# Second expert product of a decoder step: expert rows as the moving operand, 512 columns at a time

## The chip, the cores and the metric

The kernel runs on one core of a Trainium2 chip. The metric is the device time of one execution in microseconds (us). Engines are named as in the profile: PE is TensorE (matmuls), PEld its weight loads, DVE is VectorE, ACT is ScalarE, POOL is GpSimd, SP is SyncE, whose queue issues the weight transfers.

## The reference

One layer of a decoder runs over 256 prompt tokens and 64 sample tokens (8 sequences of 8), with a model width of 2048. In outline:

```
h = x + W_out [ RMSNorm(attention(q,k,v)) ; RMSNorm(SGU(u,v)) ]
h = h + PEER(RMSNorm(h))
h = h + (p @ W_ple) * sigmoid(RMSNorm(h) @ W_gate)

def one_block(xb):                       # PEER
    ...                                  # 8 heads, top 16 of 128x128 experts -> e, softmax -> g
    ue  = take(u_tab, e)                 # 16384 experts, 2048 wide
    act = gelu(einsum('thkd,td->thk', ue, xb))
    ve  = take(v_tab, e)
    return einsum('thk,thkd->td', g * act, ve)
```

The change is in the last line, the sum over experts of `g * act` times the expert's row in `v_tab`, for the 256 prompt tokens.

## The kernel before

Everything is f32 and is kept transposed: model dimensions on the 128 partitions, tokens along the free axis. `hT` holds h as 16 chunks of 128 dimensions by 320 tokens (256 prompt, then 64 sample). A weight unit is 1 MB (128 x 2048 f32); `unit` loads it through SP's queue into one of three `w_raw` buffers, and `split` makes a high part (`w_hi`, ACT, line 77) and a low part (`w_lo`, DVE, line 78) of each half of it, four buffers each, so that two units lie ready ahead of PE. `mm3` (lines 87 to 91) does a product as three matmuls: high by high, high by low, low by high. `hilo` splits an activation in the same way.

For the prompt tokens the experts are not gathered. The first product, `u_unit`, computes all 16384 activations, one unit of 128 experts at a time. Its later form (lines 612 and 613) streams the high and the low half of x in one matmul of 512 columns, and then 256 columns against `w_lo`. `weights` multiplies the activations with the dense routing weights, which are zero for experts not chosen, and splits them into `wh` and `wl`: 128 experts on partitions, 256 tokens along the free axis.

The second product, `v_group`, runs 16 times, each time for 8 units of 128 experts. It has 8 units of expert rows, each with two blocks of 128 model dimensions. For each block 24 matmuls add up in one PSUM tile `ps_o`: the expert rows are the stationary operand, 256 columns of `wh` or `wl` move. DVE then adds the tile to `hT` (line 786). Between two groups lie six or seven units of the first product.

The 64 sample tokens do gather: `c_step` fetches a row per token and choice with an indirect transfer on POOL's queue (tile `row`, two buffers) and works it up on DVE (lines 735 and 743), paced so that all 128 steps are issued when the last group starts; `add_samples` turns the sum back with matmuls against `stack` (line 772). After the last group come the per-layer embedding (`ps_s`, 96 matmuls of 320 columns, line 825 copies it out), the norm of h (`hilo` and a sum of squares for each of the 16 chunks, lines 109, 114, 133 and 134), and the gate product of 16 units.

The order of instructions on each engine is set by a scheduler with a cost model of its own, not by the program's order alone: at the start of the last group, for instance, the matmuls of `add_samples` stand among those of `ps_o`, and the norm's work on chunk after chunk stands among the products of the last group. PSUM has four tags of two banks each: `mm`, `s`, `o`, `tr`.

Of the kernel before, what the change touches and what calls it, by code (L numbers as in the profile page):

```python
# [10 lines left out]
F32 = mybir.dt.float32  # L11
# [5 lines left out]
AF = mybir.ActivationFunctionType  # L17
# [3 lines left out]
P = 128  # L21
D = 2048
NC_ = D // P
TP = 256
# [9 lines left out]
GRP = 8  # L34
NG = NK // GRP
# [13 lines left out]
def _build(ctx, tc, nc, a):  # L49
    vec, act, pool, pe = nc.vector, nc.scalar, nc.gpsimd, nc.tensor  # L50
# [5 lines left out]
    def shut(cm):  # L56
        cm.__exit__(None, None, None)
# [4 lines left out]
    ps = ctx.enter_context(tc.tile_pool(name="ps", bufs=2, space=bass.MemoryType.PSUM))  # L62
    drm = ctx.enter_context(tc.tile_pool(name="drm", bufs=1, space=bass.MemoryType.DRAM))
    gd = drm.tile([NG, P, 16 * GRP * 16], F32, name="gd")

    def psum(tag, cols, parts=P):
        t = ps.tile([P, 512], F32, tag=tag, name="ps_" + tag)
        return t[:parts, :cols]


    def split(src, lo_eng=None):
        out = []
        for h in range(2):
            hi = hl.tile([P, 8, P], F32R, name="w_hi")
            lo = hl.tile([P, 8, P], F32R, name="w_lo")
            s = src[:, 8 * h : 8 * h + 8]
            act.activation(hi, s, AF.Copy)  # L77
            (lo_eng or vec).tensor_sub(lo, s, hi.bitcast(F32))  # L78
            out.append((hi, lo))
        return lambda c: (out[c // 8][0][:, c % 8], out[c // 8][1][:, c % 8])  # L80

    def unit(src, lo_eng=None):
        r = raw.tile([P, 16, P], F32, name="w_raw")
        nc.sync.dma_start(r.rearrange("p a b -> p (a b)"), src)
        return split(r, lo_eng)

    def mm3(out, w, xh, xl, start, stop):
        wh, wl = w
        pe.matmul(out, wh, xh, start=start, stop=False)  # L89
        pe.matmul(out, wh, xl, start=False, stop=False)  # L90
        pe.matmul(out, wl, xh, start=False, stop=stop)  # L91

    def dense(out, w, x, n=NC_):
        for c in range(n):
            mm3(out, w(c), *x(c), c == 0, c == n - 1)
# [33 lines left out]
    def square_sum(pool_, tot, x, first):  # L129
        if first:  # L130
            return act.activation(tot, x, AF.Square)
        sq = pool_.tile([P, T], F32, tag="sq", name="sq", bufs=2)
        act.activation(sq, x, AF.Square)
        return vec.tensor_add(tot, tot, sq)
# [14 lines left out]
    ident = cp.tile([P, P], F32, name="ident")  # L149
    hT = cp.tile([P, NC_, T], F32, name="hT")  # L150
# [86 lines left out]
    for b4 in range(2):  # L237
        pt = psum("tr", 512)
# [225 lines left out]
    with tc.tile_pool(name="wo", bufs=2, reuse_waits="tile") as wo:  # L464

        early = [psum(tag, T) for tag in ("mm", "mm", "o", "o")]
        for half in range(2):
            for o2 in range(2):
                w = unit(a["w_out"][2 * half + o2])
                for k in range(2):  # L470
                    for c in range(8):
                        i = 8 * half + c
                        mm3(early[2 * o2 + k], w(8 * k + c), *xmix(i), i == 0, i == NC_ - 1)
        for o in range(NC_):
            xr = wo.tile([P, T], F32, name="xr", bufs=4)
            pool.dma_start(xr, a["xT"][o])
            if o < 4:
                pt = early[o]
            else:
                pt = psum("mm", T)  # L480
                dense(pt, unit(a["w_out"][o]), xmix)
            vec.tensor_add(hT[:, o], pt, xr)
            hilo(xh(o), hT[:, o], g_ffn[:, o : o + 1])
            square_sum(wo, ssq, hT[:, o], o == 0)
    shut(c_b)
    shut(c_a1)

# [24 lines left out]
    r = rstd(rt, pm[:, 0 : TP + 3], TP + 3)  # L512
# [68 lines left out]
    for n, h in enumerate((0, 4, 1, 5, 2, 6, 3, 7)):  # L581
        sp = [psum("s", 256), psum("tr", 256), psum("o", 256)]
        r0 = 64 * (h // 4)
        for half in range(2):
            pt = psum("mm", T)
# [131 lines left out]
    c_vp, vp = open_pool("vp")  # L717
# [30 lines left out]
    def paced():  # L748
        state["unit"] += 1
        while state["n"] < min(128, state["unit"] * 128 // N_UNITS):  # L750
            c_step()
# [15 lines left out]
    def add_samples():  # L767
        for c4 in range(2):
            pt = psum("tr", 512)
            for c in range(8):  # L770
                dt = 8 * c4 + c
                pe.matmul(pt[:, c * TS : c * TS + TS], acc[:, dt * P : dt * P + P], stack, start=True, stop=True)
            vec.tensor_add(
                hT[:, 8 * c4 : 8 * c4 + 8, TP:], hT[:, 8 * c4 : 8 * c4 + 8, TP:],
                pt.rearrange("p (c t) -> p c t", c=8),
            )

    def v_group(g, ws):
        for d2 in range(8):
            w = unit(a["v_t"][g, d2])  # L780
            for k in range(2):
                pt = psum("o", TP)
                for i in range(GRP):
                    mm3(pt, w(8 * k + i), *ws[i], i == 0, i == GRP - 1)
                dt = 2 * d2 + k
                vec.tensor_add(hT[:, dt, 0:TP], hT[:, dt, 0:TP], pt)
            paced()
            if g == NG - 1 and d2 == 1:
                add_samples()

    u_unit(U1, False)
    ws = weights(0)
    for e in range(U1 + 1, LEAD):
        u_unit(e, False)
    done = LEAD
    for g in range(NG):
        v_group(g, ws)
        if g + 1 < NG:
            upto = LEAD + (NK - LEAD) * (g + 1) // (NG - 1)
            while done < upto:  # L800
                if done == upto - 1 and upto < NK:
                    ws = weights(g + 1)
                u_unit(done, True)
                paced()
                done += 1
            if upto == NK:
                ws = weights(g + 1)
# [5 lines left out]
    with tc.tile_pool(name="pl", bufs=2, reuse_waits="tile") as pl:  # L813
# [17 lines left out]
        r = rstd(pl, pm, T)  # L831
        for o in range(NC_):
            pt = psum("mm", T)
# [55 lines left out]
def _layout(i):  # L889
    c = np.ascontiguousarray  # L890
    x = np.concatenate([i["x_prompt"][0], i["x_sample"].reshape(TS, D)], 0)
    p = np.concatenate([i["p_prompt"][0, 0], i["p_sample"][0].reshape(TS, -1)], 0)
    w_in = i["w_in"][0]

    order = np.concatenate([np.r_[j * HD : j * HD + HD, (8 + j) * HD : (9 + j) * HD] for j in range(NJ)])
    w_in = np.concatenate([w_in[:, order], w_in[:, 1024:]], 1)
    w_out = np.concatenate([i["w_out"][0][order], i["w_out"][0][1024:]], 0)

    first = w_out[:, :512].reshape(2, 8, P, 2, 2, P).transpose(0, 3, 2, 4, 1, 5).reshape(4, P, D)
    cols = lambda v: v.reshape(-1, P).T  # L900
    gains = np.concatenate(
        [cols(i["norm_mix"][0]), cols(i["norm_ffn"][0]), cols(i["ple_gate_norm"][0]),
         cols(i["attn_out_norm"][0][order]), cols(i["sgu_out_norm"][0]),
         np.tile(i["q_norm"][0], 2)[:, None], np.tile(i["k_norm"][0], 2)[:, None], i["sgu_norm"][0][:, None]], 1)
    sinks = i["sinks"][0].reshape(2, NJ)
    sw = i["sgu_w"][0]
    wS = np.zeros((DB, DS, SH, DB, DS), np.float32)
    for b in range(DB):
        wS[b, :, :, b, :] = sw[:, :DS, :DS].transpose(2, 0, 1)
    u, v = i["peer_u"][0], i["peer_v"][0]  # L910
    return {
        "xT": c(x.T).reshape(NC_, P, T),
        "gains": c(gains),
        "w_in": _units(w_in, 26),
        "w_out": c(np.concatenate([first, _units(w_out, 16)[4:]], 0)),
        "wq": _units(i["peer_wq"][0], 16),
        "w_gate": _units(i["ple_gate_w"][0], 16),
        "ple_w": c(i["ple_w"][0].reshape(2, P, 2, 8, P).transpose(2, 1, 3, 0, 4)).reshape(2, P, D),
        "pT": c(p.T.reshape(2, P, T).transpose(1, 0, 2)),
        "uT": c(u.reshape(NK, P, NC_, P).transpose(0, 3, 2, 1)).reshape(NK, P, D),  # L920
        "v_t": c(v.reshape(NG, GRP, P, 8, 2, P).transpose(0, 3, 2, 4, 1, 5)).reshape(NG, 8, P, D),
        "u_rows": u,
        "v_rows": v,
        "k12": c(np.stack([i["peer_k1"][0].T, i["peer_k2"][0].T], 1)),
        "ckT": c(i["cache_k"][0].transpose(2, 3, 0, 1)).reshape(P, DB, P),
        "cv": c(i["cache_v"][0].transpose(1, 0, 2, 3)).reshape(P, DB, P),
        "cache_k": i["cache_k"][0].reshape(DB, P, P),
        "cache_v": i["cache_v"][0].reshape(DB, P, P),
        "sink_p": c(np.broadcast_to(sinks.T.reshape(1, 16), (P, 16))),
        "sink_s": c(np.repeat(sinks.reshape(16), 8)[:, None]),  # L930
        "sgu_wT": c(sw.transpose(2, 0, 1)),
        "sgu_wS": wS.reshape(TS, SH, TS),
        "sgu_b": c(np.broadcast_to(i["sgu_b"][0][None], (P, SH, P))),
        "g_row": c(np.broadcast_to(i["sgu_norm"][0][None], (TS, P))),
        **_constants(),
    }
# [27 lines left out]
```

## Time and profile before

| | |
|---|---|
| time, median of 3 runs | 2170.55 us (2168.24 to 2172.44) |
| the profiled execution | 2172.83 us |
| its span, first to last instruction | 2171.1 us |
| granted PE clock, mean | 0.998 |
| busy: PE, DVE, ACT, POOL | 99%, 78%, 48%, 12% |
| traffic | 531.39 MB, mean 245 GB/s |

The span is what the views of the trace divide up; 1.7 us of the profiled execution lie outside it. Busy PE time counts a matmul from its start to its end, and matmuls overlap, so the pace of PE is read from start to start.

### The profile page before, as it was taken

How to read it: one execution, taken by the hardware profiler on the slowest of the kernel's cores; microseconds unless marked ns; L12 is line 12 of the kernel's file. 1: busy time of each engine (PE TensorE's matmuls, PEld its weight loads, DVE VectorE, ACT ScalarE, POOL GpSimd, SP SyncE). 2: the span in 40 equal slices, each digit the busy share in tenths (PEclk: the TensorE clock that was granted, in tenths of full speed). 3: DMA queues.
4: the chain of work that ended last, by engine and by line, in shares of the span. 5: the costliest groups of instructions: out<-in, count | busy, mean ns of one | idle time of the engine just before them, and what ended most of it. 6: DMA issues, size and time to landing. Idle time of an engine off the chain costs nothing.

```text
span 2171.1 us, 38182 instructions
## 1 busy us (share of the span) xinstructions
PE 2148.3 (99%) x15538; PEld 2039.2 (94%) x15538; DVE 1698.9 (78%) x2806; ACT 1034.7 (48%) x1543; POOL 263.4 (12%) x190
## 2 busy tenths in 40 slices
PE   7999999999999999999999999999999999999999
PEld 7778999999999999999999999999999999999999
DVE  6575875699988678888878888788888888788754
ACT  5246554335476644444445444444444444445632
POOL 3000000000001111111111111111212211111000
PEclk9999999999999999999999999999999999999999
DMA  7322355333567789788788878888788888886452
GB/s 266 133 78 81 104 199 179 138 117 136 176 193 238 225 312 342 293 316 317 300 316 315 309 289 318 307 323 321 289 321 303 305 310 317 299 317 253 172 178 85
DMA packets 80415, 531.39 MB, mean 245 GB/s; under 512 B 9094, under 2 KB 13622, under 8 KB 19424
## 3 DMA queue, kind: packets, MB, share of 16 engines
q1 hardware_dynamic: 50208, 350.80, 45.5%
q0 software_dynamic: 24912, 158.30, 19.5%
q10 hardware_dynamic: 5120, 19.86, 2.4%
q8 instruction: 122, 2.00, 0.4%
q14 instruction: 53, 0.43, 0.1%
HBM read 509.07 MB, written 20.84 MB: 244 GB/s over the span
## 4 chain that ended last, share of the span: by engine, by line
PE 89%; issue 5%; DVE 2%; DMA 1%; POOL 1%; ACT 0%; POOLq 0%; ACTq 0%; DVEq 0%
PE ps_mm L612 16%; PE ps_o L89 11%; PE ps_o L90 11%; PE ps_o L91 11%; PE ps_mm L90 8%; PE ps_mm L613 8%; PE ps_mm L89 8%; PE ps_mm L91 8%; PE ps_s L684 1%; POOL gd L694 1%; DVE w_lo L78 1%; DMA g_t<-gd 0%; PE ps_s L262 0%; PE ps_s L590 0%; DMA gd<-g_st 0%
## 5 line engine op out<-in xcount | busy, mean ns | idle before, releaser
L77 ACT ACTIVATE w_hi<-w_raw 128x1024 fp32r<-128x1024 f32 x664 | 703.0, 1060 | 927.4 <-PE ps_o L90 336.9
L78 DVE TENSOR_TENSOR w_lo<-w_raw,w_hi 128x1024 fp32r<-128x1024 f32 x664 | 808.8, 1223 | 253.5 <-ACT w_hi L77 249.7
L89 PE MATMUL ps_o<-wh,w_hi 128*128 128x256 f32 x2048 | 575.1, 281 | 0.6 <-ACT wh L109 0.6
L90 PE MATMUL ps_o<-wl,w_hi 128*128 128x256 f32 x2048 | 573.3, 280 | 1.0 <-DVE wl L112 1.0
L91 PE MATMUL ps_o<-wh,w_lo 128*128 128x256 f32 x2048 | 569.8, 278 | 0.3 <-DVE w_lo L78 0.3
L90 PEld LDWEIGHTS ps_o<-wl,w_hi 128*128 128x128 f32 x2048 | 385.0, 188 | 1.4 <-DVE wl L112 1.4
L89 PEld LDWEIGHTS ps_o<-wh,w_hi 128*128 128x128 f32 x2048 | 384.5, 188 | 1.6 <-ACT wh L109 1.0
L91 PEld LDWEIGHTS ps_o<-wh,w_lo 128*128 128x128 f32 x2048 | 385.0, 188 | 0.5 <-DVE w_lo L78 0.5
L89 PE MATMUL ps_mm<-a,w_hi 128*128 128x320 f32 (+1 forms) x1008 | 310.1, 308 | 9.0 <-ACT w_hi L77 8.9
L90 PE MATMUL ps_mm<-a,w_hi 128*128 128x320 f32 (+1 forms) x1008 | 311.9, 309 | 0.7 <-DVE a L114 0.7
L91 PE MATMUL ps_mm<-a,w_lo 128*128 128x320 f32 (+1 forms) x1008 | 308.1, 306 | 1.8 <-DVE w_lo L78 1.8
L612 PE MATMUL ps_mm<-a,w_hi 128*128 128x512 f32 x768 | 270.9, 392 | 0.0
L612 PE MATMUL ps_mm<-c,w_hi 128*128 128x512 f32 x768 | 270.8, 391 | 0.0
L613 PE MATMUL ps_mm<-c,w_lo 128*128 128x256 f32 x768 | 215.1, 280 | 0.0
L613 PE MATMUL ps_mm<-a,w_lo 128*128 128x256 f32 x768 | 215.1, 280 | 0.0
L89 PEld LDWEIGHTS ps_mm<-a,w_hi 128*128 128x128 f32 x1008 | 191.8, 190 | 14.4 <-ACT w_hi L77 9.1
L90 PEld LDWEIGHTS ps_mm<-a,w_hi 128*128 128x128 f32 x1008 | 192.0, 190 | 9.1 <-issue 7.6
L91 PEld LDWEIGHTS ps_mm<-a,w_lo 128*128 128x128 f32 x1008 | 191.6, 190 | 5.3 <-issue 2.6
L612 PEld LDWEIGHTS ps_mm<-c,w_hi 128*128 128x128 f32 x768 | 143.7, 187 | 31.8
L612 PEld LDWEIGHTS ps_mm<-a,w_hi 128*128 128x128 f32 x768 | 143.7, 187 | 31.3
L730 POOL DMA_INDIRECT row<-in_v_rows,c_e x64 | 111.3, 1740 | 496.2 <-DVE xc L743 440.6
L730 POOL DMA_INDIRECT row<-in_u_rows,c_e x64 | 101.1, 1580 | 509.3 <-DVE row L735 503.2
(338 smaller groups left out, 3144.2 us busy)
## 6 DMA issues: line engine op xcount, KB each, us to landing
w_raw<-in_uT SPq DMA_DIRECT2D x128, 1024.0 KB
w_raw<-in_v_t SPq DMA_DIRECT2D x128, 1024.0 KB
w_raw<-in_w_in SPq DMA_DIRECT2D x25, 1024.0 KB
w_raw<-in_w_out SPq DMA_DIRECT2D x16, 1024.0 KB
w_raw<-in_wq SPq DMA_DIRECT2D x16, 1024.0 KB
gd<-g_st POOLq DMA_DIRECT2D x16, 1024.0 KB, 6.1
g_t<-gd ACTq DMA_DIRECT2D x16, 1024.0 KB
w_raw<-in_w_gate SPq DMA_DIRECT2D x16, 1024.0 KB
```

The lines of the kernel that those rows point to most:

```text
L77: act.activation(hi, s, AF.Copy)
L78: (lo_eng or vec).tensor_sub(lo, s, hi.bitcast(F32))
L89: pe.matmul(out, wh, xh, start=start, stop=False)
L90: pe.matmul(out, wh, xl, start=False, stop=False)
L91: pe.matmul(out, wl, xh, start=False, stop=stop)
L612: pe.matmul(pt, wh, x(c), start=c == 0, stop=False)
L613: pe.matmul(pt[:, 0], wl, x(c)[:, 0], start=False, stop=c == NC_ - 1)
L684: pe.matmul(gp[:, t * P : t * P + P], e2[:, q, :, t], p[:, q, :, t], start=k == 0, stop=k == 1)
L694: pool.dma_start(gd[:, :, tb * P : tb * P + P].rearrange("g p x -> p g x"), st.rearrange("p (g i) t -> p g (i t)", g=NG),)
L730: pool.indirect_dma_start(out=row, out_offset=None, in_=tab, in_offset=bass.IndirectOffsetOnAxis(ap=c_e[:, j : j + 1], axis=0),)
```

## The change

The operands of the second product change places. Stationary is now a block of 128 experts by 128 tokens of `wh` or `wl`; moving are 512 model dimensions of the expert rows. Sums stand with tokens on partitions, and `hT`'s prompt columns serve as their accumulator: group 0 copies into it, groups 1 to 15 add. So h itself is written to DRAM (`hd`) when it is made, read back into the two `row` buffers at the start of the last group, and added to the sums when those are turned back by PE transposes (`h_back`), a quarter of the model width at a time. The rows in `v_t` are laid out anew; its units keep their size.

```diff
+    hd = drm.tile([2, P, 8 * TP], F32, name="hd")
...
-    def split(src, lo_eng=None):
+    def split(src, lo_eng=None, wide=1):
...
+        if wide > 1:
+            return lambda i: [x[:, i * wide % 8 : i * wide % 8 + wide].rearrange("p a b -> p (a b)") for x in out[i * wide // 8]]
...
             square_sum(wo, ssq, hT[:, o], o == 0)
+            if o % 8 == 7:
+                pool.dma_start(hd[o // 8], hT[:, o - 7 : o + 1, 0:TP])
...
+    def y_part(tt, dq):
+        return hT[:, 4 * dq : 4 * dq + 4, tt * P : tt * P + P]
+
+    def h_back(dq):
+        for c in range(4 * dq, 4 * dq + 4, 2):
+            pt = psum("tr", 512)
+            for k in range(4):
+                pe.transpose(pt[:, k * P : k * P + P], hT[:, c + k // 2, k % 2 * P : k % 2 * P + P], ident)
+            vec.tensor_add(
+                hT[:, c : c + 2, 0:TP], h_kept[c // 8][:, c % 8 : c % 8 + 2], pt.rearrange("p (c t) -> p c t", c=2)
+            )
+
     def v_group(g, ws):
-        for d2 in range(8):
-            w = unit(a["v_t"][g, d2])
-            for k in range(2):
-                pt = psum("o", TP)
-                for i in range(GRP):
-                    mm3(pt, w(8 * k + i), *ws[i], i == 0, i == GRP - 1)
-                dt = 2 * d2 + k
-                vec.tensor_add(hT[:, dt, 0:TP], hT[:, dt, 0:TP], pt)
-            paced()
-            if g == NG - 1 and d2 == 1:
-                add_samples()
+        for dq in range(4):
+            pt = [psum("o", 512), psum("s", 512)]
+            for ih in range(2):
+                w = unit(a["v_t"][g, 2 * dq + ih], wide=4)
+                for i in range(4):
+                    wh, wl = w(i)
+                    e = 4 * ih + i
+                    for tt in range(2):
+                        xh_, xl_ = [x[:, tt * P : tt * P + P] for x in ws[e]]
+                        pe.matmul(pt[tt], xh_, wh, start=e == 0, stop=False)
+                        pe.matmul(pt[tt], xl_, wh, start=False, stop=False)
+                        pe.matmul(pt[tt], xh_, wl, start=False, stop=e == GRP - 1)
+                paced()
+            for tt in range(2):
+                y, p = y_part(tt, dq), pt[tt].rearrange("p (c d) -> p c d", c=4)
+                if g == 0:
+                    act.activation(y, p, AF.Copy)
+                else:
+                    vec.tensor_add(y, y, p)
+            if g == NG - 1:
+                if dq == 0:
+                    add_samples()
+                h_back(dq)
...
     for g in range(NG):
+        if g == NG - 1:
+            h_kept = []
+            for k in range(2):
+                t = vp.tile([P, D], F32, tag="row", name="h_kept", bufs=2)
+                nc.scalar.dma_start(t, hd[k])
+                h_kept.append(t.rearrange("p (c t) -> p c t", c=8))
         v_group(g, ws)
...
-        "v_t": c(v.reshape(NG, GRP, P, 8, 2, P).transpose(0, 3, 2, 4, 1, 5)).reshape(NG, 8, P, D),
+        "v_t": c(v.reshape(NG, 2, 4, P, 4, 512).transpose(0, 4, 1, 3, 2, 5)).reshape(NG, 8, P, D),
```

## Rows read from the trace of the kernel before

**Rows 1.** The page: span, PE's busy time, and the chain that ended last.
```profile
span 2171.1 us, 38182 instructions
...
PE 2148.3 (99%) x15538; PEld 2039.2 (94%) x15538; DVE 1698.9 (78%) x2806; ACT 1034.7 (48%) x1543; POOL 263.4 (12%) x190
...
PE 89%; issue 5%; DVE 2%; DMA 1%; POOL 1%; ACT 0%; POOLq 0%; ACTq 0%; DVEq 0%
```

**Rows 2.** Busy time by stretch: group 0, group 8, units after it, group 15; sum of 1000:1900.
```profile
core 0: us, PE busy (x) PEld busy (x) DVE busy (x) ACT busy (x) POOL busy (x), PEclk, DMA share, GB/s
775.58:823.17 47.59, 45.98 (x385) 45.18 (x385) 45.05 (x72) 22.55 (x32) 5.25 (x4) 1.00 0.86 326
...
1422.91:1468.14 45.23, 45.23 (x387) 45.23 (x385) 37.95 (x42) 19.27 (x24) 10.19 (x6) 1.00 0.82 297
1468.14:1501.42 33.28, 33.28 (x194) 29.34 (x193) 27.47 (x34) 16.29 (x25) 5.05 (x3) 1.00 0.87 316
1989.14:2037.82 48.68, 48.68 (x418) 48.49 (x417) 43.10 (x69) 30.99 (x51) 0.00 (x0) 1.00 0.50 174
...
sum 900.00, PE 900.00 PEld 852.32 DVE 738.22 ACT 409.13 POOL 160.92; mean PE 100.00 PEld 94.70 DVE 82.02 ACT 45.46 POOL 17.88
```

**Rows 3.** Waits from 775 to 1990: total us, times, longest.
```profile
ACT w_hi L77 <- PE ps_o L90: 317.7, 184, 2.3
...
ACT w_hi L77 <- DMA w_raw<-in_v_t: 2.2, 1, 2.2
...
PE ps_o L90 <- DVE wl L112: 1.0, 2, 0.8
```

**Rows 4.** The chain from 1468.2 to 1501.3, six units of the first product, by line.
```profile
by line: PE ps_mm L612 66.1%; PE ps_mm L613 34.1%; PE ps_o L91 0.4%
```

**Rows 5.** Timeline of PE in the gate product: start, us; 48 matmuls apart.
```profile
2100.02 0.31 PE L89 MATMUL ps_mm<-c,w_hi 128*128 128x320 f32 x1
...
2107.06 0.31 PE L89 MATMUL ps_mm<-c,w_hi 128*128 128x320 f32 x1
```

**Rows 6.** Groups of instructions from 1989 to 2060: busy, mean ns, idle before.
```profile
L78 DVE TENSOR_TENSOR w_lo<-w_raw,w_hi 128x1024 fp32r<-128x1024 f32 x23 | 28.0, 1221 | 9.9 <-ACT w_hi L77 9.9
...
L134 DVE TENSOR_TENSOR ssq<-ssq,sq 128x320 f32<-128x320 f32 x15 | 7.3, 484 | 0.1
...
L786 DVE TENSOR_TENSOR hT<-hT,ps_o 128x256 f32<-128x256 f32 x16 | 6.6, 415 | 0.5 <-PE ps_o L91 0.3
...
L114 DVE SCALAR_TENSOR_TENSOR c<-hT,c_gains,c 128x320 fp32r<-128x320 f32 x8 | 4.4, 545 | 0.0
...
L773 DVE TENSOR_TENSOR hT<-hT,ps_tr 128x512 f32<-128x512 f32 x2 | 1.4, 684 | 1.1 <-PE ps_tr L772 1.1
```

**Rows 7.** Timeline of PE: six transposes of f32, and what follows.
```profile
194.73 0.88 PE L220 MATMUL ps_tr<-ident,hT 128*128 128x128 f32 x6
195.36 0.39 PE L89 MATMUL ps_mm<-a,w_hi 128*128 128x320 f32 x1
```

**Rows 8.** Timeline of DVE after the last group: last add, last chunk, last of rstd.
```profile
2038.21 0.41 DVE L786 TENSOR_TENSOR hT<-hT,ps_o 128x256 f32<-128x256 f32 x1
...
2040.61 0.48 DVE L134 TENSOR_TENSOR ssq<-ssq,sq 128x320 f32<-128x320 f32 x1
...
2050.77 0.49 DVE L126 SCALAR_TENSOR_TENSOR rs_y<-rs_x,rs_y 128x320 f32<-128x320 f32 x1
```

**Rows 9.** Timeline of PE after the last group: embedding's first and last matmul.
```profile
2037.82 0.31 PE L89 MATMUL ps_s<-p_h,w_hi 128*128 128x320 f32 x1
...
2054.70 0.31 PE L91 MATMUL ps_s<-p_h,w_lo 128*128 128x320 f32 x1
```

**Rows 10.** Timeline of POOL in the output projection: a load of x.
```profile
317.95 0.54 POOL L476 DMA_DIRECT2D xr<-in_xT  x1 [6.50 <-DVE hT L482]
```

**Rows 11.** Timeline of DVE in the output projection: the eighth and ninth add.
```profile
338.29 0.49 DVE L482 TENSOR_TENSOR hT<-ps_mm,xr 128x320 f32<-128x320 f32 x1 [1.30 <-PE ps_mm L91]
...
345.32 0.49 DVE L482 TENSOR_TENSOR hT<-ps_mm,xr 128x320 f32<-128x320 f32 x1 [1.30 <-PE ps_mm L91]
```

**Rows 12.** The page's DMA issues: KB each, median us to landing.
```profile
gd<-g_st POOLq DMA_DIRECT2D x16, 1024.0 KB, 6.1
```

**Rows 13.** Timeline of DVE at the start of the last group: last `row`, last `wl`.
```profile
1991.84 2.35 DVE L743 SCALAR_TENSOR_TENSOR xc<-row,c_w,xc 128x2048 f32<-128x2048 f32 x1
...
1995.00 0.43 DVE L112 TENSOR_TENSOR wl<-act,wh 128x256 fp32r<-128x256 f32 x1 [0.48 <-ACT wh L109]
```

More of the change, by code (lines that the diff above doesn't have):

```diff
@@ L79, in split, with unit @@
             out.append((hi, lo))
+        if wide > 1:
+            return lambda i: [x[:, i * wide % 8 : i * wide % 8 + wide].rearrange("p a b -> p (a b)") for x in out[i * wide // 8]]
         return lambda c: (out[c // 8][0][:, c % 8], out[c // 8][1][:, c % 8])
-    def unit(src, lo_eng=None):
+    def unit(src, lo_eng=None, wide=1):
         r = raw.tile([P, 16, P], F32, name="w_raw")
         nc.sync.dma_start(r.rearrange("p a b -> p (a b)"), src)
-        return split(r, lo_eng)
+        return split(r, lo_eng, wide)
     def mm3(out, w, xh, xl, start, stop):
```

## The prediction

> **What bounds the kernel now.** I read the page first: PE is busy for 99% of the span and holds 89% of the chain that ended last [rows 1]. That says who, not why, so I asked for stretches. From 1000 to 1900 us PE is never idle, DVE is busy 82%; in one steady group and the units behind it PE is at 100%, its clock granted at 1.00 (the 2.4 GHz level), the transfers at 0.82 to 0.87 of the DMA engines' time [rows 2]. The waits say the same from the other side: ACT waits 317.7 us for PE to free split buffers, 2.2 us for a unit of expert rows to land; PE's largest wait here is 1.0 us in all [rows 3]. So between 775 and 2038 us time is what PE needs to stream its matmuls, start to start. The durations of 280 or 390 ns that the page gives are of no use for that, since matmuls overlap; the pace must come from the length of a stretch and the number of matmuls that the code puts in it.
>
> **The pace.** A group of the second product has 8 x 2 x 24 = 384 matmuls of 256 columns and takes 45.23 us: 117.8 ns each. Six units of the first product have 96 pairs of 512 and 256 columns and take 33.28 us: 346.7 ns a pair [rows 2]. A pair streams the 768 columns of three matmuls of the second product, which take 353.4 ns. The only difference in number is that two matmuls of 256 are one of 512, and it is worth 6.7 ns. The chain splits the pair: 66.1 to 34.1, so 228.7 ns for the 512 columns and 118.0 for the 256 [rows 4]; by that, two of 256 less one of 512 is 6.9 ns. The columns are what costs, and their number doesn't change; only the small part that each matmul costs by itself is halved.
>
> **The change part by part.**
>
> *Matmuls.* 16 x 384 = 6144 of 256 columns become 16 x 4 x 2 x 4 x 2 x 3 = 3072 of 512: 3072 mergers. At 6.7 ns that is 20.5 us less, the value I take, since the pair is the same operation with the same type and the same split buffer in it. The bounds come from the matmuls of 320 columns, which follow each other at (2107.06 - 2100.02) / 48 = 146.7 ns [rows 5]. The line through 256 and 320 columns has 0.451 ns a column and gives 233.3 ns at 512, so only 2.2 ns a merger, 6.8 us. If instead the 13.3 ns by which 320 columns exceed their time at 2.4 GHz stay the same at 512, a matmul takes 226.7 ns, and a merger saves 8.9 ns, 27.4 us.
>
> The Trainium skill (TensorE: Matmul & The Clock Gate, section "Back-to-back issue gap") gives N / 2.4 + 2.5 ns between matmuls of N columns in a stream. By its figure a merger would save 2.5 ns, an estimate of 7.7 us in place of 20.5. The trace differs: it has 117.8 ns where that rule has 109.2.
>
> *Group 0.* It took 47.59 us, 2.4 more than a steady one [rows 2], with waits for `wh` and `wl` among its first matmuls: its first block runs through all eight pairs in 24 x 0.118 = 2.8 us. After the change a pair feeds six matmuls of 0.229, and all eight are asked for over 11 us. I take 1.5 us off; bounds 0 and 2.4. In the last group the last `wl` ends at 1995.4, 6.3 us after its start [rows 13, 2]; the new order asks for it after 7 x 1.37 = 9.6 us.
>
> *Evictions.* 256 adds of 256 columns at 415 ns become 120 of 512 and eight copies on ACT. An add of 512 from PSUM takes 684 ns [rows 6], so DVE gets back 256 x 0.415 - 120 x 0.684 = 24 us, and nothing of it shows, since DVE's 18% of idle time is already PE's cover. A quarter takes PE 11 us and has two banks of each tag, so an eviction has 11 us to spare. The copies stand on ACT, busy 45%. The order in which units free their split buffers stays half by half, at 2.75 us a half against 2.83.
>
> *h to DRAM.* Two transfers of 1 MB on POOL's queue, behind chunks 7 and 15. A transfer of that size landed in 6.1 us [rows 12]. If the first stands ahead of the load of x for chunk 8, that load goes out at 338.8 and not at 317.95 [rows 10, 11] and lands some 7 us later, about when the add at 345.3 wants it; if it is late by 2 us, the second bank of `mm` gives PE 7 us more. Without that second bank it would cost those 2 us. The second transfer stands ahead of constants that nothing asks for before expert choice. Nothing, then.
>
> *h back.* Two transfers of 1 MB on ACT's queue, which must wait for the last two `row` buffers, free at 1994.2 [rows 13]. ACT's next work then, the last `wh`, waits for the same DVE queue, and two split units lie ready, so I price it at nothing; with 6.1 us of landing they are there at about 2000.5, when the first quarter of the group (from 1989.1, 11 us) ends. In that stretch DMA is at 0.50 [rows 2].
>
> *Turning back.* 32 transposes. Six take from 194.73 to 195.36: 0.105 us each [rows 7]; 3.4 us of PE. Bounds 2.2 and 4.5 (two of the six have 64 columns only). In the first three quarters the next quarter's matmuls can stand around them.
>
> *The end.* Before, after the last add the last chunk's norm was done 2.9 us later (2038.21 to 2041.09) and the inverse root 13.1 us later [rows 8], both under the embedding's matmuls, 2037.82 to 2054.85, in which some of the gate's already stood [rows 9]. Now the last quarter adds, after its last matmul, two adds of 0.68 in place of one of 0.41, eight transposes (0.84), two adds back (1.4), and four chunks in place of one, each 0.55 + 0.48 on DVE [rows 6]: (1.37 - 0.41) + 0.84 + 1.4 + 3.1 = 6.3 us later. The embedding's 96 x 0.1467 = 14.1 us still cover it: the last chunk is wanted at 14, and is ready at 2.9 + 6.3 and a `w_lo` or two of 1.2 us, some 11. The inverse root is wanted two gate units later. I take 1 us; bounds 0 and 6 (all of the delay).
>
> *Sum.* -20.5 - 1.5 + 3.4 + 1 = -17.6 us. The profiled execution took 2172.83 us, 2171.1 of it span, and is 2.3 us above the median shown; on it 2155.2, on the scale of the median **2153**.
>
> **The rivals.**
>
> *Columns are all that costs.* The 512-column matmul goes by the line through 256 and 320 columns: 6.8 us saved, less the end's 4.4, plus 1.5: 3.9 faster, 2166.6. For it: that line, and that a pair's 346.7 ns is 0.451 a column to the third digit. Against it: the chain's 228.7 for the very form. Chance 0.14. The figure of the Trainium skill cited above (TensorE: Matmul & The Clock Gate, "Back-to-back issue gap") would lead to almost the same time, an estimate of 2166.
>
> *The matmul's own part is larger.* 226.7 ns, so 27.4 saved: 2146. For it: 320 columns and the pair both show 13.3 ns a matmul over 2.4 GHz. Against it: 256 columns show 11.1. Chance 0.12.
>
> *The last group stalls.* PE's order puts each quarter's transposes right behind its matmuls. Then PE stands for two adds behind a `w_lo`, a chunk and a sum of squares in DVE's queue: 1.37 + 1.22 + 0.55 + 0.48 = 3.6 us, three times; and if the embedding is placed ahead of the last quarter, the end loses its cover and PE waits for 10 us of chunks and part of the inverse root's 9.7. With the transposes: 10.8 + 10 + 9 + 3.4 = 33 against the 22 saved: 11 slower, 2182. It decides once the last group and the end cost more than 22 + 4.3 = 26.3 us. For it: DVE in that group needs, per 11 us, 4 x 1.22 + 4 x 0.68 + 4 x 1.03 = 11.7 us, more than there is. Against it: in the old last group the matmuls of the samples stand among those of `ps_o` without PE idling; 48.68 us is 45.23 and 32 short matmuls. Chance 0.07.
>
> **How the numbers follow.** The forecast, 2147 to 2162 in its own range (its terms between their bounds, not all at one end), has the remaining 0.67. With all terms at their worst (6.8 saved, 0, 4.5, 6) it would be 3.7 slower, 2174; at their best 27.6 faster, 2143. The range 2144 to 2168 leaves out the stalled end, the upper half of the column rival and the tip of the other, some 2 in 10. A measurement here can tell about 0.2%, 4.3 us. Faster by more than that: the forecast nearly whole, the larger own part, and a part of the column rival, 0.82; within it 0.11; slower 0.07.
>
> **What would show it.** A group of the second product should take 192 x 0.229 = 44.0 us in place of 45.2, at 3072 matmuls, and the chain's share of it falls with it; the six units behind group 8 stay at 33.3. If a group takes 44.8, the column rival is right; 43.5, the larger part. Group 0 should be within 1 us of the others. In the last group 32 transposes of 0.1 us should stand among matmuls, with no wait of PE for DVE above 1 us; from its end to the first matmul of an unbroken gate product 14 to 18 us. The prediction is wrong if PE waits for `h_kept`, for the adds back or for `w_lo` after the last group, or if waits of `w_hi` for transfers appear between groups, which would mean that the transfers, at 0.87, had become the pace.

## The result, and the profile after

The changed kernel takes 2181.32 us (median of 4 runs, 2179.49 to 2182.84) against 2169.81 us for the kernel before, measured beside it: a ratio of 1.0051, 95% interval 1.0039 to 1.0062. It is 0.5% slower where I forecast 0.8% faster.

The page of the changed kernel says as little about the cause as that of before [rows 1]; PE is as busy and its share of the chain is smaller:

```profile
span 2177.7 us, 31857 instructions
...
PE 2150.9 (99%) x12498; PEld 1894.9 (87%) x12498; DVE 1686.3 (77%) x2678; ACT 1043.1 (48%) x1551; POOL 268.8 (12%) x192
...
PE 82%; issue 9%; DMA 3%; DVE 3%; POOL 1%; ACT 0%; DVEq 0%; POOLq 0%; ACTq 0%
```

Cut into stretches at the start of group 0, the two traces compare like this (us; each number is a stretch between two starts on PE):

| | before | after | difference |
|---|---|---|---|
| up to group 0 | 775.6 | 770.4 | -5.2 |
| groups 0 to 14 of the second product | 680.4 | 681.8 | +1.4 |
| the fifteen stretches of units between them | 533.2 | 540.4 | +7.2 |
| last group to the end | 181.9 | 185.2 | +3.3 |

The first line is not the change's: between 40 and 75 us the granted clock was 0.90 in the profiled execution of before and 1.00 in that of after. PE's 300th matmul starts 5.06 us earlier in the latter (61.31 against 66.37 us), its 5000th, long behind the transfers of h to DRAM, 5.07 us earlier (719.38 against 724.45). From group 0 on the changed kernel is 11.9 us slower, and that is what the medians show too (11.5).

The windows of the changed kernel that answer to [rows 2], columns as there: group 8, six units behind it, group 9, seven units behind that, group 14, and the last group with the embedding.

```profile
1420.07:1464.88 44.81, 44.81 (x194) 36.10 (x193) 38.11 (x39) 20.20 (x26) 9.73 (x6) 1.00 0.92 331
1464.88:1498.17 33.29, 33.29 (x194) 29.09 (x192) 26.42 (x29) 15.88 (x23) 5.03 (x3) 1.00 0.74 266
1498.17:1545.11 46.94, 45.05 (x194) 35.99 (x193) 38.88 (x37) 20.18 (x26) 10.80 (x6) 1.00 0.90 341
1545.11:1584.68 39.57, 39.57 (x226) 34.34 (x224) 29.63 (x33) 18.60 (x27) 5.03 (x3) 1.00 0.70 260
1903.94:1953.67 49.73, 46.40 (x194) 37.07 (x193) 36.42 (x33) 18.14 (x21) 10.05 (x6) 0.97 0.85 319
1992.50:2060.72 68.22, 68.22 (x363) 58.09 (x362) 58.34 (x80) 42.73 (x74) 0.00 (x0) 1.00 0.51 191
```

Four things are to be seen. A group without waits takes 44.81 us, 0.42 less than before, where I had 44.0: 233.3 ns for 512 columns, the number of the column rival. Two groups lose 2.1 and 4.9 us. Seven units, which took 38.83 us before, take 39.57 with PE busy throughout: 353.3 ns a pair, not 346.7; eight of the fourteen stretches after the first are like that, and none of these fourteen was before. And the last stretch, 65.70 us before (1989.14 to 2054.84), is 2.5 us longer.

The trace of before has two rows, though, that I had not used: the units behind group 0, and group 1.

```profile
823.17:857.09 33.92, 33.92 (x195) 29.41 (x193) 30.02 (x46) 16.59 (x25) 5.05 (x3) 1.00 0.89 335
857.09:901.90 44.81, 44.81 (x387) 44.81 (x385) 36.45 (x44) 19.23 (x24) 7.27 (x5) 1.00 0.78 290
```

With PE never idle, the pairs took 353.3 ns there, and the 384 matmuls of 256 columns 116.7 ns each in place of 117.8. So both streams had two paces already in the kernel before, and group 1 with 256 columns took as long as a group with 512 does now. Group 0 ran at 116.7 ns too, after its first eighth.

The two slow groups are waits. The waits of the changed kernel from 765 to 1995 (us in total, times, longest):

```profile
ACT w_hi L78 <- DMA w_raw<-in_v_t: 29.4, 11, 3.6
...
DVE xc L749 <- DMA row<-in_v_rows,c_e: 17.3, 7, 6.6
...
DVE row L741 <- DMA row<-in_u_rows,c_e: 10.8, 7, 3.1
...
PE ps_o L810 <- DVE w_lo L79: 7.1, 3, 3.3
```

Before, DVE never waited for a gathered row in this time, and for units there were 2.2 us of waiting [rows 3]. The longest case stands in group 14, on DVE:

```profile
1906.64 2.34 DVE L749 SCALAR_TENSOR_TENSOR xc<-row,c_w,xc 128x2048 f32<-128x2048 f32 x1
1915.55 2.35 DVE L749 SCALAR_TENSOR_TENSOR xc<-row,c_w,xc 128x2048 f32<-128x2048 f32 x1 [6.58 <-DMA row<-in_v_rows,c_e]
1917.82 3.49 DVE L79 TENSOR_TENSOR w_lo<-w_raw,w_hi 128x1024 fp32r<-128x1024 f32 x3
```

and on PE, a little later:

```profile
1915.37 0.40 PE L809 MATMUL ps_o<-w_hi,wl 128*128 128x512 f32 x1
1919.10 0.80 PE L810 MATMUL ps_o<-w_lo,wh 128*128 128x512 f32 x1 [3.33 <-DVE w_lo L79]
1919.69 0.63 PE L808 MATMUL ps_s<-w_hi,wh 128*128 128x512 f32 x1
1920.11 0.63 PE L809 MATMUL ps_s<-w_hi,wl 128*128 128x512 f32 x1
```

DVE stands for 6.58 us at a row whose gather is still under way, with three `w_lo` queued behind it; the two split units that I counted on as cover run out, and PE stands 3.33 us. What follows costs as well: after the pause 512 columns come 0.42 us apart instead of 0.233, for some 2.9 us. The granted clock of the whole stretch is 0.97, and here it is at the 1.2 GHz level:

```profile
1918.60:1922.00 3.40, 2.90 (x7) 2.35 (x8) 3.40 (x5) 0.00 (x0) 1.25 (x1) 0.50 0.45 111
```

### The profile page after: what moved, and what is told of

Read it like the earlier page. It is cut to its first block, busy times and chain, and to the rows that moved or that the text cites. A ratio compares the mean times of both kernels' runs of the same rounds, so it can differ in the third digit from the quotient of the medians.

```text
span 2177.7 us, 31857 instructions
## 1 busy us (share of the span) xinstructions
PE 2150.9 (99%) x12498; PEld 1894.9 (87%) x12498; DVE 1686.3 (77%) x2678; ACT 1043.1 (48%) x1551; POOL 268.8 (12%) x192
## 4 chain that ended last, share of the span: by engine, by line
PE 82%; issue 9%; DMA 3%; DVE 3%; POOL 1%; ACT 0%; DVEq 0%; POOLq 0%; ACTq 0%
PE ps_mm L618 14%; PE ps_mm L93 8%; PE ps_mm L92 8%; PE ps_mm L94 8%; PE ps_mm L619 7%; PE ps_o L810 5%; PE ps_s L809 5%; PE ps_s L810 5%; PE ps_s L808 5%; PE ps_o L808 5%; PE ps_o L809 5%; DMA row<-in_v_rows,c_e 2%; DVE w_lo L79 1%; DMA g_t<-gd 1%; POOL gd L700 1%
## 5 line engine op out<-in xcount | busy, mean ns | idle before, releaser
L810 PE MATMUL ps_o<-w_lo,wh 128*128 128x512 f32 x512 | 203.6, 398 | 7.1 <-DVE w_lo L79 7.1
L808 PE MATMUL ps_o<-w_hi,wh 128*128 128x512 f32 x512 | 203.3, 397 | 0.2 <-ACT wh L112 0.2
L809 PE MATMUL ps_s<-w_hi,wl 128*128 128x512 f32 x512 | 203.0, 397 | 0.0
L809 PE MATMUL ps_o<-w_hi,wl 128*128 128x512 f32 x512 | 202.8, 396 | 0.1
L808 PE MATMUL ps_s<-w_hi,wh 128*128 128x512 f32 x512 | 202.6, 396 | 0.0
L810 PE MATMUL ps_s<-w_lo,wh 128*128 128x512 f32 x512 | 202.6, 396 | 0.0
```

The costliest lines, as they stand in the source:

```text
L808: pe.matmul(pt[tt], xh_, wh, start=e == 0, stop=False)
L809: pe.matmul(pt[tt], xl_, wh, start=False, stop=False)
L810: pe.matmul(pt[tt], xh_, wl, start=False, stop=e == GRP - 1)
```

## The experiments

The times of single stretches are from the traces; ratios are to the kernel before, run beside it. Since the first 775 us vary with dips of the clock by up to 7 us, I also give the time from the start of group 0 to the end: 1395.5 us before, 1407.4 after.

**The changed kernel once more**, no edit.

> The changed kernel once more, nothing edited. In its first trace eight of the fourteen stretches of first-product units between two groups ran at 353.3 ns a pair (33.92 and 39.57 us in place of 33.28 and 38.83), and PE waited 1.9 and 3.3 us for a late w_lo in two groups. Theory that the order of the program sets both: the same stretches are slow and the same groups wait, span 2176 to 2180. Rival, that they fall by chance of the execution: other stretches, other groups, and their number may change by several.

2184.02 us; 1409.0 from group 0. Windows of three stretches of units, behind groups 1, 8 and 9:

```profile
900.81:934.73 33.92, 33.92 (x194) 29.43 (x192) 24.72 (x30) 16.01 (x23) 4.62 (x3) 1.00 0.75 280
...
1469.88:1503.16 33.28, 33.28 (x193) 29.09 (x192) 26.43 (x29) 15.89 (x23) 5.04 (x3) 1.00 0.75 267
1548.91:1588.48 39.57, 39.57 (x225) 34.34 (x224) 29.63 (x33) 18.61 (x27) 5.04 (x3) 1.00 0.72 259
```

Eleven of fourteen stretches are slow: the same eight, behind groups 2, 3, 4, 6, 7, 9, 11 and 12, and three more (the first row was at 33.28 in the first trace). Group 14 waits in both, group 9 too, and group 3 only here. Neither theory is right by itself: the program's order fixes most of it, the execution the rest.

**512 columns cut in two.** Loads and matmuls at 6144 again, operands as in the change.

```diff
-                        pe.matmul(pt[tt], xh_, wh, start=e == 0, stop=False)
-                        pe.matmul(pt[tt], xl_, wh, start=False, stop=False)
-                        pe.matmul(pt[tt], xh_, wl, start=False, stop=e == GRP - 1)
+                        for st, mv, a0, a1 in (
+                            (xh_, wh, e == 0, False), (xl_, wh, False, False), (xh_, wl, False, e == GRP - 1),
+                        ):
+                            for q in (slice(0, 256), slice(256, 512)):
+                                pe.matmul(pt[tt][:, q], st, mv[:, q], start=a0 and q.start == 0, stop=a1 and q.start == 256)
```

> The changed kernel with every 512-column matmul of the second product issued as two of 256 columns against the same stationary block, so loads and matmuls are back at 6144 with the new operands. Theory that columns are what costs, and a merger is worth 2.2 ns: a group takes 45.2 us in place of 44.8, the whole 7 us more than the changed kernel, about 1.008 of the kernel before. Rival, that a merger is worth 6.7 ns as I predicted and the new operand order lost that elsewhere: a group takes 46.1, the whole 20 us more, 1.015. If the 512-column matmuls ahead of them are what slows the units of the first product, these return to 33.28 and 38.83 us, 6 us less.

1.0104 (1.0083 to 1.0126); 1415.5 us from group 0. Group 8, and the units behind it:

```profile
1425.24:1470.68 45.44, 45.44 (x387) 45.44 (x385) 37.90 (x39) 20.20 (x26) 9.74 (x6) 1.00 0.91 331
1470.68:1504.60 33.92, 33.92 (x195) 29.41 (x193) 26.29 (x29) 15.88 (x23) 5.04 (x3) 1.00 0.73 261
```

A group costs 0.63 us more than with 512 columns: a merger is worth 0.63 / 192 = 3.3 ns here, half of what I took. And at equal widths the new operand order is slower than the old: 118.3 ns for 256 columns against 117.8 (and 116.7). The width is not what slows the units; twelve of their fourteen stretches behind groups 1 to 14 are slow.

**The place the price came from.** The kernel before, its pairs undone.

```diff
-                pe.matmul(pt, wh, x(c), start=c == 0, stop=False)
-                pe.matmul(pt[:, 0], wl, x(c)[:, 0], start=False, stop=c == NC_ - 1)
+                pe.matmul(pt[:, 0], wh, x(c)[:, 0], start=c == 0, stop=False)
+                pe.matmul(pt[:, 1], wh, x(c)[:, 1], start=False, stop=False)
+                pe.matmul(pt[:, 0], wl, x(c)[:, 0], start=False, stop=c == NC_ - 1)
```

> The kernel before with the first product's later units issued as three matmuls of 256 columns in place of one of 512 and one of 256: 1536 mergers undone at the place from which I took the price. Theory that the pair's pace of 346.7 ns is worth 6.7 ns a merger there, whatever it is worth elsewhere: triples of 353.4, six units take 33.9 us, 10 us slower, 1.0047. Rival, 2.2 ns a merger everywhere, the rest being a pace that the pairs may or may not have: 349 a triple, 3.4 us slower, 1.0016.

1.0076 (1.0054 to 1.0097); 1415.9 us from group 0. Group 8, and six units:

```profile
1431.89:1477.12 45.23, 45.23 (x386) 45.23 (x385) 37.73 (x42) 19.25 (x24) 9.96 (x6) 1.00 0.80 295
1477.12:1511.68 34.56, 34.56 (x291) 34.56 (x289) 27.54 (x34) 16.28 (x25) 5.04 (x3) 1.00 0.86 307
```

Both expectations were too low: 34.56 / 288 = 120.0 ns a matmul, so the pair saves 13.3 ns there. The same three matmuls on the same columns cost 117.8 ns each in the second product and 120.0 in the first. I had set a pair of one product against three matmuls of the other; that difference is not the price of a merger in either.

**A third row buffer** in the changed kernel (two fewer `act`, one fewer `wh` and `wl` to make room).

```diff
-        row = vp.tile([P, D], F32, name="row", bufs=2)
+        row = vp.tile([P, D], F32, name="row", bufs=3)
```

> The changed kernel with three row buffers in place of two, so that a gather can be issued a step earlier (paid for by two fewer act buffers and one fewer wh and wl). Theory that DVE stands at a row that its order puts ahead of several w_lo, while the gather is still under way: DVE's waits for gathers fall from 28 us to under 5, PE's waits for w_lo from 7 us to under 1, the whole 7 to 9 us less than the changed kernel, about 2173, 1.001 of the kernel before. Rival, that w_lo is late because the new evictions or the transfers of units hold it up: the waits stay at 5 us or more and the time at 2180.

2176.06 us against 2168.9 before; 1.0027 (1.0015 to 1.0038); 1404.4 from group 0. No wait of DVE for a gathered row is left, and groups 9 and 14 take 44.80 and 44.79 us. What PE still waits for `w_lo` stands in group 0 and right behind it:

```profile
PE ps_mm L619 <- DVE w_lo L79: 2.5, 1, 2.5
...
PE ps_o L810 <- DVE w_lo L79: 2.1, 2, 1.9
```

So the waits in groups 9 and 14 were gathers that DVE's order asked for too soon. The groups sum to 675.5 us, 6.3 less than in the first trace of the change; the stretch behind group 0 gave 2.5 back, and the whole stayed above the 2173 us expected. The prediction had named waits of `w_hi` for transfers as a sign that the transfers set the pace. They are still here:

```profile
ACT w_hi L78 <- DMA w_raw<-in_v_t: 28.0, 11, 3.4
```

They were 29.4 us in the first trace of the change, and with nearly as many now groups 9 and 14 lose nothing. So they were not what held PE there.

**Without turning back.** `hd`, `h_kept` and `h_back` are left out; y is then made from the sums as they lie and without h of the prompt tokens.

```diff
-                pool.dma_start(hd[o // 8], hT[:, o - 7 : o + 1, 0:TP])
...
-                h_back(dq)
```

> The changed kernel without keeping h in DRAM, reading it back and turning the sums back: y is then made from the sums as they lie, without h of the prompt tokens. Theory that the end costs what 32 transposes take and nothing waits: 3 to 4 us less than the changed kernel, 2177, 1.0035. Rival, that the turning back stalls the last group or the transfers of h disturb the first stages: 8 us less or more, 1.001 and below.

1.0055 (1.0033 to 1.0076), no gain in the median, where 1.0035 was expected; this kernel's profiled execution had its dips of the clock ahead of group 0 (777.35 us up to there). From the last group on it takes 181.40 us, the change 185.20:

```profile
2001.10:2182.50 181.40, 176.54 (x1092) 166.64 (x1090) 111.62 (x150) 81.19 (x121) 0.00 (x0) 0.99 0.41 145
```

So the turning back costs 3.8 us, within the 3 to 4 expected. The median alone would not have shown it.

**The second product as pairs, in the old operand order.** The kernel before; `wh` and `wl` lie side by side in one tile.

```diff
-                    mm3(pt, w(8 * k + i), *ws[i], i == 0, i == GRP - 1)
+                    wh, wl = w(8 * k + i)
+                    pe.matmul(pt, wh, ws[i], start=i == 0, stop=False)
+                    pe.matmul(pt[:, 0], wl, ws[i][:, 0], start=False, stop=i == GRP - 1)
...
-                vec.tensor_add(hT[:, dt, 0:TP], hT[:, dt, 0:TP], pt)
+                for half in range(2):
+                    vec.tensor_add(hT[:, dt, 0:TP], hT[:, dt, 0:TP], pt[:, half])
```

> The kernel before with the second product in the pair form of the first: expert rows stay stationary, wh and wl lie side by side and move as one matmul of 512 columns against w_hi, then wh alone against w_lo; DVE adds both halves of the tile, 256 more adds of 0.42 us. Theory that the pair form is what has the price of 346.7 in place of 353.4: a group takes 128 x 0.3467 = 44.4 us, 13.7 us less in all, 0.994, if DVE at 82% plus 5 points keeps w_lo in time. Rival, that pairs run at 353.3 here as in the slow stretches: groups stay at 45.2 and the time is that of before or, with DVE's added work, some us more.

1.0089 (1.0067 to 1.011). The waits of PE in it (765 to 2000):

```profile
PE ps_o L785 <- ACT w_hi L77: 11.5, 11, 1.1
PE ps_o L785 <- DVE hT L789: 7.3, 9, 1.3
PE ps_o L785 <- DVE whl L112: 2.2, 2, 1.4
```

PE now stands for evictions and for `w_hi`. Two banks with two adds each in DVE's queue were too few, or DVE was. The next run tells which.

**The same with four banks.**

```diff
-                pt = psum("o", 2 * TP).rearrange("p (a t) -> p a t", a=2)
+                pt = psum("os"[k], 2 * TP).rearrange("p (a t) -> p a t", a=2)
```

> The kernel before with the second product in the pair form, as in the last such run, but with its tiles taken in turn from tags o and s, four banks in place of two. In that run the pairs had their pace (the stretches of pure streaming sum to 13.7 us less than before) and lost over 20 us to waits in PE for w_hi and for evictions. Theory that the two banks, with two adds each, are the tight place: the waits go and the time is 2158 to 2162, 0.995. Rival, that DVE at 87% is: the waits stay and the time is 2180 or more.

2160.06 us against 2168.9; 0.9954 (0.9936 to 0.9972): faster than both kernels. Group 8 and six units:

```profile
1417.03:1461.41 44.38, 44.38 (x258) 39.34 (x257) 42.00 (x56) 19.20 (x24) 9.35 (x6) 1.00 0.81 305
1461.41:1494.70 33.29, 33.29 (x195) 29.35 (x193) 28.78 (x36) 16.34 (x25) 5.04 (x3) 1.00 0.85 314
```

What is left of PE's waits at the second product from 765 to 2000, and the sum of the engines over 1000 to 1900:

```profile
PE ps_o L785 <- DVE whl L112: 2.2, 2, 1.4
```

```profile
sum 900.00, PE 900.00 PEld 795.77 DVE 803.36 ACT 412.83 POOL 144.76; mean PE 900.00 PEld 795.77 DVE 803.36 ACT 412.83 POOL 144.76
```

A group is 128 pairs of 346.7 ns, and with DVE at 89% (803.36 of 900 us) PE waits nowhere from 1000 to 1900: it was the banks. Against the steady groups of before (45.23 us) a merger gives 0.85 / 128 = 6.6 ns here; against group 1 (44.81) half of that. From group 0 on the kernel takes 1383.2 us, 12.3 less than before, and 0.6 of that is the stretch behind group 0, which runs at 346.7 ns a pair here.

**The same stationary block twice in a row** in the changed kernel: the second and third matmul of each triple exchanged (xh by wh, xh by wl, xl by wh).

> The changed kernel with the second and third matmul of each triple exchanged, so that two neighbours have the same stationary block (wh, wh, wl), as the kernel before had (w_hi, w_hi, w_lo). Theory that a 512-column matmul costs 233.3 ns whatever is loaded before it: groups stay at 44.8 us, the time at 2181. Rival, that a repeated stationary block is worth some ns, which the change gave away: groups of 44.3 or less, 7 us or more off.

1.0077 (1.0058 to 1.0096); groups without waits stay at 44.79 to 44.82 us. Which of the blocks stands twice in a row makes no difference. From group 0 on it takes 6.2 us more than the change: PE's waits for `w_lo` are longer (10.0 us against 7.8), and eleven stretches are slow in place of eight.

**One triple of the other form ahead of the units**, in either kernel, with a spare tile that nothing uses but a one-column copy.

```diff
+                extra = psum("tr", TP)                      # after
+                mm3(extra, (wh[:, 0:P], wl[:, 0:P]), *ws[7], True, True)
...
+                for x in (ws[7][0], ws[7][1], ws[7][0]):    # before; extra of 512 columns
+                    pe.matmul(extra, x[:, 0:P], wide, start=True, stop=True)
```

> The changed kernel with one triple in the old form (expert rows stationary, 256 columns moving, into a spare tile that ACT reads one column of) at the end of groups 0 to 14, just ahead of the units of the first product. Theory that the pace of a whole stretch of pairs is set by what stands right ahead of it: all stretches run at 346.7 ns a pair, 33.28 and 38.83 us, as in the kernels with the old form; 5 us for the triples, 6 us back. Rival, that it is not the last matmuls but something that lasts (the phase in which the stretch begins, the state of the queues): eight to ten of the fourteen are slow as before, time at 2185.

> The counterpart: the kernel before with one triple in the new form (a block of wh or wl stationary, 512 columns of expert rows moving, into a spare tile) at the end of groups 0 to 14. Theory that what stands right ahead sets the pace: about half of the stretches or more fall to 353.3 ns a pair, 33.92 and 39.57 us, 5 us, besides 0.7 us for each triple (10 us), 2186. Rival: all stretches stay at 33.28 and 38.83, 2180.

2183.09 and 2180.04 us, one run each, against 2172.58 for the kernel before. The seven units behind group 9, first in the changed kernel with the old triple, then in the old one with the new triple:

```profile
1547.21:1586.78 39.57, 39.57 (x227) 34.34 (x225) 29.29 (x33) 18.69 (x28) 5.03 (x3) 1.00 0.73 264
```

```profile
1550.01:1588.84 38.83, 38.83 (x226) 33.96 (x224) 31.92 (x36) 18.69 (x28) 9.52 (x4) 1.00 0.80 292
```

Nine of fourteen slow there, none here. A triple of the other form right ahead of a stretch does not set its pace.

**Widths in turn.** The changed kernel with the low-part matmul cut in two and set between the others.

```diff
-                        pe.matmul(pt[tt], xl_, wh, start=False, stop=False)
-                        pe.matmul(pt[tt], xh_, wl, start=False, stop=e == GRP - 1)
+                        pe.matmul(pt[tt][:, 0:256], xh_, wl[:, 0:256], start=False, stop=False)
+                        pe.matmul(pt[tt], xl_, wh, start=False, stop=False)
+                        pe.matmul(pt[tt][:, 256:], xh_, wl[:, 256:], start=False, stop=e == GRP - 1)
```

> The changed kernel with the low-part matmul of each triple cut into two of 256 columns and set between the others, so that 512 and 256 columns alternate as in the pairs of the first product: 256 matmuls a group in place of 192, the same columns. Theory that the pair's pace belongs to the alternation of widths and not to the saved matmul: two pairs of 346.7 ns in place of three matmuls of 233.3, a group takes 44.4 us in place of 44.8, or 45.2 if the pairs run at 353.3. Rival, that every matmul has its own cost of some 2 to 3 ns: 64 more matmuls a group, 44.95 to 45.0 us.

1.0099 (1.0079 to 1.0118). Group 8 and six units:

```profile
1427.99:1473.22 45.23, 45.23 (x259) 39.28 (x257) 38.04 (x39) 20.14 (x25) 9.75 (x6) 1.00 0.90 330
1473.22:1507.13 33.91, 33.91 (x194) 29.42 (x193) 26.51 (x29) 15.92 (x23) 5.03 (x3) 1.00 0.74 264
```

128 pairs at 353.3 ns, and all fourteen stretches of units are slow. The same widths in the same turn take 346.7 ns with the expert rows stationary (four banks, above) and 353.3 with them moving. Alternation alone is not the fast pace. Whether the operand order has a part in it is not shown: this run also adds its two matmuls of 256 columns to different halves of the tile.

## Why the prediction was wrong

**The step that failed is the first term, the matmuls.** I priced a merger at 6.7 ns, from a pair of the first product against three matmuls of the second, and got 20.5 us. Against the steady groups of before it measured 0.42 us a group, 2.2 ns a merger, 5.5 us over groups 2 to 14; against group 1 (44.81 us) it measured nothing. That was my lower bound, and the column rival to the decimal: 233.3 ns at 512 columns is the line through 256 and 320 columns [rows 2, 5].

What I had compared were two paces. Three matmuls of the second product take 353.4 ns at their slower pace and 350.0 at the faster one, a pair of the first 353.3 or 346.7. I took the slower pace of the one and the faster of the other, and called the difference the price of a merger; the two faster ones give 3.3 ns. For pairs in the old operand order 6.7 ns was about right, as the four-bank kernel shows against the steady groups. In the new order a merger is worth 3.3 ns, and changing the order takes some of that back. What I used against the column rival, the chain's split of the pair into 228.7 and 118.0 ns [rows 4], cannot bear it: in the changed kernel the same view over a stretch at 346.7 ns (898 to 931 us) gives 67 to 33, some 232 and 115. The sum of a pair is firm, its split is not.

The prediction gives the rule of the Trainium skill (TensorE: Matmul & The Clock Gate, section "Back-to-back issue gap") for matmuls in a stream, where that section gives it for a matmul by itself. No term of the sum rests on it.

**Two losses I had not priced.** The units of the first product, which I left at 33.3 us a stretch, lost 5.5 us to the pace of 353.3 ns in eight stretches. And groups 9 and 14 lost 7 us at rows that DVE waited for. I had counted DVE's idle 18% as PE's cover and never asked where its order would put the 128 row steps once the evictions came every 11 us instead of every 2.8; the third buffer, with which these waits are gone, shows that rows asked for ahead of their gather were the cause. That the new spacing of the evictions moved them there is not shown. The stretch right behind group 0, with 35.56 us against 33.92, makes up the rest.

**Group 0** gained 0.2 us, 47.37 in place of 47.59, all of it in its first eighth, where it loses 2.6 us and lost 2.8 before. The waits moved from `wh` and `wl` to `w_lo`, 1.86 us of it in one piece. The 1.5 us that I took off were wrong.

**The end was right.** I had 4.4 us for transposes and delay; it is 3.3 more in the table, and 3.8 by the run without them. The transposes stand among matmuls, as forecast, and after the last quarter among the embedding's:

```profile
2008.67 0.60 PE L793 MATMUL ps_tr<-ident,hT 128*128 128x128 f32 x4
2009.03 0.48 PE L808 MATMUL ps_o<-w_hi,wh 128*128 128x512 f32 x1
...
2043.57 0.31 PE L92 MATMUL ps_s<-p_h,w_hi 128*128 128x320 f32 x1
...
2043.86 0.39 PE L793 MATMUL ps_tr<-ident,hT 128*128 128x128 f32 x2
```

PE did not wait for DVE in this part. So the stalling rival fell. That its sign was the right one, and its 2182 us lie next to the 2181.32 measured, is chance: the kernel is slower by another mechanism. **h to DRAM and back** cost nothing that shows: the lead of 5.06 us that the changed kernel has at the 300th matmul is 5.07 at the 5000th, with the writing of h between them, and PE waits for nothing in the last group.

Summed from group 0 on: -5.5 for the pace in groups 2 to 14, -0.2 in group 0, +7.1 of waits in groups 3, 9 and 14, +7.2 in the units, +3.3 in the last group and the end: 11.9 us slower. The sign turned on all of it; without the waits and the slow units the change would have been 2.4 us faster, near nothing.

**What stays open** is why the same matmuls have two paces, 6.7 ns a pair apart, with PE never idle. It is not the width of the matmuls in the group, not the triple right ahead, and not the banks (the four-bank kernel uses the tags `o` and `s` too, and its stretches are fast). It is not the operand order alone either. The stretch behind group 0 was slow in the kernel before, and in the two-bank kernel, whose rows are stationary, four of fifteen stretches were, behind groups 0, 11, 12 and 13. This is 80 pairs of the one behind group 11:

```profile
1731.53:1759.79 28.26, 28.26 (x163) 24.52 (x161) 23.01 (x27) 14.51 (x23) 5.59 (x4) 1.00 0.92 355
```

Those four, and none of the other eleven, begin with a pair that is torn apart: matmuls of the second product stand between its two. And in the run with 512 columns cut in two the stretch behind group 0 changed its pace on the way, 40 pairs of 353.3 ns first and 47 of 346.7 at the end:

```profile
819.16:833.29 14.13, 14.13 (x82) 12.26 (x81) 11.22 (x21) 7.75 (x14) 0.53 (x1) 1.00 0.76 290
836.74:853.03 16.29, 16.29 (x96) 14.36 (x95) 14.88 (x18) 7.93 (x12) 3.36 (x2) 1.00 0.99 380
```

The faster pace begins right behind one matmul of 512 columns that took 0.39 us, start to start, in place of 0.24. That looks like a rhythm which the stream keeps until something breaks it, but no run was made to show that. In the kernel before, the four-bank kernel and the one with an added triple, the fourteen stretches behind groups 1 to 14 were fast; in each kernel with the rows moving, eight to fourteen of these were slow, mostly the same ones. Where operands lie, and what DVE, ACT and the transfers do beside them, was not tried.

## What to carry to other kernels

When PE streams without a pause and the columns stay the same in number, a change of shape is worth a few ns a matmul at most, and that price depends on the pattern: take it from the same operands in the same roles, and from every stretch of them, since the same matmuls can run at two paces (group 1 of the kernel before took 44.81 us, the thirteen behind it 45.23). Or take the bound that assumes columns are everything. With thousands of matmuls the small term decides the sign, so first try the cheaper edit that keeps the operand roles: here pairs in the old order and two more banks gave 0.5%, with no turning back. And a queue that is idle 18% of the time is no cover by itself; what counts is what stands in it ahead of the instruction that the busy engine needs, and whether that can be late.

## What the runs showed of the hardware

At the 2.4 GHz level 256 columns of f32 took 116.7 or 117.8 ns a matmul in streams of the second product as it was before, 118.3 with the rows moving, and 120.0 in the first product; 320 took 146.7, 512 took 233.3; a pair of 512 and 256 took 346.7 or 353.3. Exchanging which stationary block stands twice in a row changed nothing (44.8 us a group). The Trainium skill (TensorE: Matmul & The Clock Gate, section "Back-to-back issue gap") gives N / 2.4 + 2.5 ns for a matmul by itself, by which 512 columns would take 215.8 ns, an estimate; in the streams here they took 233.3, and the measurement decides. From 256 to 512 columns a column cost (233.3 - 117.8) / 256 = 0.451 ns. A pause of PE of 3.33 us was followed by some 2.9 us of matmuls at the 1.2 GHz level (granted clock 0.50), 0.42 us for 512 columns. The dips of the granted clock in the first 300 us (0.90 to 1.00 between 40 and 75 us) differ between executions of like programs and moved the start of group 0 by up to 7 us.
